# The output norm of a fused decoder layer: three engines or VectorE alone, and one addition moved between two products

## The chip, the cores and the metric

One core of a Trainium2 chip runs the whole layer. The metric is the device time of one execution in microseconds (us); of several runs the median is given. The engines named here: TensorE (PE in the profile; its weight loads are PEld) multiplies, VectorE (DVE), ScalarE (ACT) and POOL (GpSimd) work elementwise, and SP issues the transfers.

## The reference, cut to what matters

The layer projects x (2048 x 2048, float32), runs a convolution branch and an attention branch, concatenates them to y and maps y back. The change touches the last two lines only:

```python
    y = jnp.concatenate([y_conv, y_attn], axis=-1)
    y = jnp.einsum("bse,ed->bsd", y, w_out) + b_out
    return layer_norm(DEEPNORM_ALPHA * x + y, ln_g, ln_b)

def layer_norm(x, g, b):
    mu = jnp.mean(xf, axis=-1, keepdims=True)
    var = jnp.mean(jnp.square(xf - mu), axis=-1, keepdims=True)
    y = (xf - mu) * lax.rsqrt(var + LN_EPS)
    return y * g + b
```

## The kernel before, in words

**Stages.** The sequence is cut into four chunks of 512 rows (`SC`, `NCH`). The list `steps` (L612 to L620) holds 4 x 84 steps of the input projection with its branches, then 112 steps of the output projection. This document is about the latter, called the output stage.

**Products.** The output projection runs by Strassen-like products: two blocks (`blk` 0 and 1) of two chunks each, and for each block seven products in the order 1, 2, 6, 5, 3, 7, 4 (`PRODS`, L33). A product has two halves (`dp` 0 and 1) of four steps (`p` 0 to 3). A step multiplies one 128 x 1024 weight piece with two tiles of y for four row tiles (`tp`): 24 matmuls, since float32 is handled as a high and a low part and each product of parts is its own matmul (`mm3`, L738 to L741). The half `dp` 0 accumulates in the right-hand banks (tiles out_s, out_t, out_v in the profile), `dp` 1 in the left-hand ones (tile out).

**Weights.** SP loads a piece (`wr`) three steps ahead (`load_w(n + 3)`). Two steps ahead `split_w` makes the high part `wh` on ScalarE (L135); the low part `wl` is loaded from DRAM in steps with even p, and in steps with odd p it is computed on POOL by `lo_part` (L138, `wl<-wr,wh`). The pieces of the last three steps are handled by `tail_w` in two halves each.

**Positions and U.** An output tile of 128 x 512 is a position; it starts as `xn`, alpha x + b_out (`scale_xn`, L432), and `evac_out` adds products to it. c11 and c12 belong to the block's first chunk, c21 and c22 to its second. U keeps product 1 (copied on ScalarE) and takes product 6, then product 7 in addition. After product 7 the tile U is added to c21 and c22, and c22 is done; c21 is done after product 4. `z_done` takes a position's statistics (`bn_stats`, L439); c11 is spilled to DRAM there and later loaded again as `zl`. The evacuations of a half are emitted in the first step of the half that follows (`late`, L878 to L883).

**The norm.** `out_norm(c)` (L583) makes 19 background functions for a chunk: one with the small per-row work (`norm_small`, L554) and the first loads, 16 units (one position each, `norm_unit`, L572) and two with the last stores. Function n of a unit also loads the position after next and stores the one before the last. A unit is three operations on three engines: ScalarE scales and shifts the rows (L575), VectorE multiplies by g (L576), POOL adds b (L577). Chunk 0 is started at the first step of product 7 in block 0, chunk 1 at the first step of block 1, chunk 2 at the first step of product 7 in block 1. The fourth chunk has a norm of its own, `tail_norm` (L753 to L783), in the last step.

**What sets the order.** Background functions wait in the queue `bg`; each step of the output stage takes one, or two if its number is a multiple of 4 or more than 18 are queued (L889). All transfers go through SP in the order in which the code emits them (`dma`, L72 to L78), so a store that waits for its data holds back the loads behind it. All 128 x 512 tiles come from one pool of 69 slots (`NSLOT`). The last four steps (from `TAIL`, L621) emit no matmuls until the last one, which runs all four for one row tile after the other, each followed by its evacuation and its norm (L897 to L903).

Of the kernel before, what the change touches and what calls it, by code (L numbers as in the profile page):

```python
# [12 lines left out]
AF = mybir.ActivationFunctionType  # L13
ALU = mybir.AluOpType
# [37 lines left out]
def hybrid_layer_kernel(ctx, tc, x, xT, w_first, w_in, w_out, consts, b_out, ln_g, ln_b, out):  # L52
    nc = tc.nc
    V, A, G, T = nc.vector, nc.scalar, nc.gpsimd, nc.tensor
# [25 lines left out]
    def slot(name, dt=F32):  # L80
        return slots.tile([P, 512], dt, tag="slot", name=name)

    def acc_bank(name):
        return ps_acc.tile([P, 512], F32, tag="acc", name=name)
# [7 lines left out]
    def score_banks(name):  # L92
        sc = ps_sc.tile([P, 2, 512], F32, tag="sc", name=f"{name}_s")
        return [sc[:, 0, :], sc[:, 1, :]]

    def right_banks(name):
        return score_banks(name) + [ps_pt.tile([P, 512], F32, tag="pt", name=f"{name}_t"),
                                    ps_pv.tile([P, 512], F32, tag="pv", name=f"{name}_v")]
# [35 lines left out]
    def copy(dst, src):  # L134
        A.activation(out=dst, in_=src, func=AF.Copy)  # L135
# [37 lines left out]
    bg = deque()  # L173
    later = []
    st = {}

    def run_bg(n):
        for _ in range(min(n, len(bg))):
            bg.popleft()()

    def run_all():
        run_bg(len(bg))
# [251 lines left out]
    def z_done(c, s, d, spill=False):  # L434

        z = st["z", c, s, d] = st.pop(("zx", c, s, d))
        if ("bn", c, s) not in st:
            st["bn", c, s] = small.tile([P, 4, 6], F32, tag="bn", name=f"bn{c}_{s}", bufs=16)
        V.bn_stats(out=st["bn", c, s][:, d, :], in_=z)  # L439
        if spill:  # L440
            t = zd[c, s, d] = dram.tile([P, 512], F32, tag=f"zd{c}_{s}_{d}", name=f"zd{c}_{s}_{d}")
            store_later(t, st.pop(("z", c, s, d)))
# [6 lines left out]
    def add(a, b):  # L449
        V.tensor_tensor(out=a, in0=a, in1=b, op=ALU.add)  # L450

    def evac_out(blk, i, dp, tp):


        ps = st["banks", dp][tp]
        c11, c12, c21, c22 = (2 * blk, tp, dp), (2 * blk, tp, dp + 2), (2 * blk + 1, tp, dp), (2 * blk + 1, tp, dp + 2)
        if i == 1:
            u = st["U", dp, tp] = slot(f"U{blk}_{dp}_{tp}")
            copy(u, ps)
            add(st["zx", *c11], ps)  # L460
        elif i == 2:
            add(st["zx", *c11], ps)
            z_done(*c11, spill=True)
        elif i == 6:
            add(st["U", dp, tp], ps)
            add(st["zx", *c12], st["U", dp, tp])
        elif i == 7:
            u = st.pop(("U", dp, tp))
            add(u, ps)
            add(st["zx", *c21], u)  # L470
            add(st["zx", *c22], u)
            z_done(*c22)
        elif i == 4:
            add(st["zx", *c21], ps)
            z_done(*c21)
        elif i == 5:
            add(st["zx", *c12], ps)
            add(st["zx", *c22], ps)
        else:
            add(st["zx", *c12], ps)  # L480
            z_done(*c12)
# [72 lines left out]
    def norm_small(c, ss):  # L554

        n = len(ss)
        mv = small.tile([P, 4, 2], F32, tag="mv", name=f"mv{c}_{ss[0]}")
        w = small.tile([P, 4, 4], F32, tag="w", name=f"w{c}_{ss[0]}")
        for k, s in enumerate(ss):
            V.bn_aggr(out=mv[:, k, :], in_=st["bn", c, s])  # L560
        V.tensor_scalar(out=w[:, 0, 0:n], in0=mv[:, 0:n, 1], scalar1=EPS, scalar2=None, op0=ALU.add)
        for f in rsqrt_steps(w[:, 0, 0:n], w[:, 1, 0:n], w[:, 2, 0:n]):
            f()
        V.scalar_tensor_tensor(out=w[:, 3, 0:n], in0=mv[:, 0:n, 0], scalar=-1.0, in1=w[:, 1, 0:n],
                               op0=ALU.mult, op1=ALU.mult)
        for k, s in enumerate(ss):
            st["nrm", s] = (w[:, 1, k:k + 1], w[:, 3, k:k + 1])

    def load_gb(c, d):
        st["g", d], st["b", d] = bcast_row(ln_g, d, f"g{c}_{d}"), bcast_row(ln_b, d, f"b{c}_{d}")  # L570

    def norm_unit(c, s, d):  # L572
        z = st["z", c, s, d]
        rstd, nmr = st["nrm", s]
        A.activation(out=z, in_=z, func=AF.Identity, scale=rstd, bias=nmr)  # L575
        V.tensor_tensor(out=z, in0=z, in1=st["g", d], op=ALU.mult)  # L576
        G.tensor_tensor(out=z, in0=z, in1=st["b", d], op=ALU.add)  # L577

    def store(c, s, d):
        r = c * SC + s * P  # L580
# [144 lines left out]
    for j in range(16):  # L725
        job = (j // 8, j // 2 % 4, j % 2)
        n = PER + 10 + 14 * j
# [10 lines left out]
    def mm3(o, lh, ll, mh, ml, start, stop):  # L738
        T.matmul(o, lh, mh, start=start, stop=False)  # L739
        T.matmul(o, lh, ml, start=False, stop=False)  # L740
        T.matmul(o, ll, mh, start=False, stop=stop)  # L741
# [57 lines left out]
    for n, s in enumerate(steps):  # L799
        st["n"] = n  # L800
        c = s[1]
# [4 lines left out]
        if c == 0 and s[0] == "first":  # L806
            i = s[2]
# [20 lines left out]
        if s[0] in ("first", "last"):  # L828
            p = s[2]
            hi, lo = splits[n]  # L830
            if p == 0 and s[0] == "first":
                st["acc"] = [acc_bank(f"in{c}_{i}") for i in range(2)] + score_banks(f"in{c}")
            elif p == 0:
                st["acc"] = right_banks(f"in{c}l")
            for t in range(4):
                for kk in range(2):
                    k = 2 * p + kk
                    xh, xl = xs[c, k]
                    if s[0] == "first":
                        h, l = (w[kk][:, t * P:(t + 1) * P] for w in (hi, lo))  # L840
                    else:
                        h, l = (w[t // 2][:, t % 2 * 256 + kk * P:t % 2 * 256 + kk * P + P] for w in (hi, lo))
                    mm3(st["acc"][t], h, l, xh, xl, k == 0, k == KT - 1)
            if p == 7 and s[0] == "first":
                for t in (2, 3, 1, 0):
                    evac_in(c, t, *ORDER[t], st["acc"][t])
            elif p == 7:
                for t in range(4):
                    evac_in(c, 38 + t, *ORDER[38 + t], st["acc"][t])
                run_all()  # L850
                bg.extend(st["fins"])
            run_bg(2)
        elif s[0] == "in":
            _, c, t, kind, j, hf = s
            hi, lo = splits[n]
            if hf == 0:
                ps = acc_bank(f"in{c}_{t}")
            for k in range(8):
                xh, xl = xs[c, hf * 8 + k]
                cols = slice(k % 4 * P, (k % 4 + 1) * P)  # L860
                mm3(ps, hi[k // 4][:, cols], lo[k // 4][:, cols], xh, xl, hf == 0 and k == 0, hf == 1 and k == 7)
            if hf == 1:
                evac_in(c, t, kind, j, ps)
            run_bg(5)
        else:
            _, blk, i, dp, p = s
            if p == 0:
                st["banks", dp] = (left_banks if dp else right_banks)(f"out{blk}_{i}_{dp}")
            for h, d in NEW.get(i, ()):
                if p == 0:  # L870
                    st["bo", d] = bcast_row(b_out, dp + d, f"bo{blk}_{i}_{dp}_{d}")
                else:
                    scale_xn(2 * blk + h, p - 1, dp + d, st["bo", d])
                load_xn(2 * blk + h, p, dp + d)
            tail = n >= TAIL
            if not tail:
                out_mm(n, range(4))
            for f, *args in late:  # L878
                f(*args)
            late = []  # L880
            if p == 3 and not tail:
                late = [(scale_xn, 2 * blk + h, 3, dp + d, st["bo", d]) for h, d in NEW.get(i, ())]
                late += [(evac_out, blk, i, dp, tp) for tp in range(4)]  # L883
            if dp == 0 and p == 0:
                if i == 7:
                    bg.extend(out_norm(2 * blk))
                elif i == 1 and blk == 1:
                    bg.extend(out_norm(1))
            run_bg(2 if n % 4 == 0 or len(bg) > 18 else 1)  # L889
            if TAIL - 6 <= n < TAIL - 3:  # L890
                tail_w(n + 7)
            if TAIL - 3 <= n < TAIL:
                st["tailw", n + 4]()
                if n == TAIL - 1:
                    for d in range(4):
                        load_gb(3, d)
            if n == len(steps) - 1:  # L897
                run_all()
                for tp in range(4):
                    for m in range(TAIL, TAIL + 4):  # L900
                        out_mm(m, (tp,))
                    evac_out(blk, i, dp, tp)
                    tail_norm(3, tp)  # L903
# [78 lines left out]
```

## Time and profile before

| | |
|---|---|
| median of 3 runs (lowest to highest) | 2689.36 us (2686.81 to 2693.9) |
| the profiled execution | 2691.23 us |
| its span, first to last instruction | 2689.2 us |
| matmuls busy, share of the span | 97% |
| VectorE, ScalarE, POOL busy | 70%, 43%, 32% |
| granted clock of TensorE, mean | 0.991 of full speed |

A duration is that of one instruction; an engine that works without a pause starts the next one somewhat before the end of the one before. "Idle before" is time in which the engine did nothing ahead of the row's instruction, with the instruction that released it. Tile names leave buffer numbers out: out_s, out_t and out_v are accumulation banks of `dp` 0, out those of `dp` 1; wr, wh and wl are a weight piece and its parts; xn and zl are positions that were kept or loaded again; yl is the low part of a tile of y.

### The profile page before, as it was taken

To read this page: it belongs to the slowest core of one execution; us is meant where nothing else is said; L and a number is where in the kernel's file an instruction comes from. 1 tells how busy PE (TensorE), PEld (TensorE's weight loads), DVE (VectorE), ACT (ScalarE), POOL (GpSimd) and SP (SyncE) were. 2 spreads that over 40 slices of the span, in tenths; PEclk is the share of its full clock that TensorE was granted. 3 is DMA by queue.
4 is the path that set the end of the run, shared out by engine and by line. 5 is a ranking of instruction groups with operands and counts; after the bars stand their busy time and mean duration, and the time that the engine had idled before them with its cause. 6 is when DMAs were issued, how large, how long until landed. Compare 5 with 4: busy or idle time off the path is not lost.

```text
span 2689.2 us, 34266 instructions
## 1 busy us (share of the span) xinstructions
PE 2616.0 (97%) x12064; PEld 2175.8 (81%) x12064; DVE 1884.6 (70%) x2992; ACT 1155.9 (43%) x2069; POOL 856.4 (32%) x582
## 2 busy tenths in 40 slices
PE   8999999999999999999999999999999999899985
PEld 7888888788888887888888888888888887678874
DVE  4487788847658757486767747657857768697687
ACT  4344344634444545344454644444444324243241
POOL 2455455312222323122222212312122224352244
PEclk9999999999999999999999999999999999899997
DMA  7655555766755687656766866755568888699894
GB/s 266 190 177 174 174 181 188 249 234 233 234 189 200 211 291 264 212 197 208 242 219 208 298 237 227 239 190 198 192 219 312 315 285 302 201 346 336 275 311 141
DMA packets 238348, 629.51 MB, mean 234 GB/s; under 512 B 26464, under 2 KB 42976, under 8 KB 238176
## 3 DMA queue, kind: packets, MB, share of 16 engines
q1 hardware_dynamic: 238176, 627.32, 68.6%
q8 instruction: 95, 1.56, 0.2%
q14 instruction: 77, 0.63, 0.1%
HBM read 513.97 MB, written 113.25 MB: 233 GB/s over the span
## 4 chain that ended last, share of the span: by engine, by line
PE 54%; DVE 5%; ACT 1%; issue 1%; DMA 1%; POOL 1%; DVEq 0%; SPq 0%; POOLq 0%; ACTq 0%
PE in L741 10%; PE in L740 10%; PE in L739 10%; PE out L740 3%; PE out L741 3%; PE out L739 3%; PE out_s L740 2%; PE out_s L741 2%; PE out_s L739 1%; PE pv L353 1%; DVE xn L450 1%; PE out_t L739 1%; PE out_t L740 1%; PE out_t L741 1%; PE out_v L739 1%
## 5 line engine op out<-in xcount | busy, mean ns | idle before, releaser
L739 PE MATMUL in<-xh,wh 128*128 128x512 f32 x2304 | 903.5, 392 | 9.5 <-ACT xh L135 6.3
L741 PE MATMUL in<-xh,wl 128*128 128x512 f32 x2304 | 898.8, 391 | 3.7 <-DMA wl<-wlo 3.7
L740 PE MATMUL in<-xl,wh 128*128 128x512 f32 x2304 | 899.8, 391 | 0.0
L135 ACT ACTIVATE wh<-wr 128x1024 fp32r<-128x1024 f32 (+1 forms) x452 | 473.0, 1049 | 809.7 <-PE in L740 313.4
L227 DVE SCALAR_TENSOR_TENSOR cv<-h,cst,cv 128x512 f32<-128x512 f32 x896 | 628.6, 747 | 2.4
L739 PEld LDWEIGHTS in<-xh,wh 128*128 128x128 f32 x2304 | 433.5, 188 | 97.5 <-ACT xh L135 7.0
L741 PEld LDWEIGHTS in<-xh,wl 128*128 128x128 f32 x2304 | 433.3, 188 | 95.2 <-DMA wl<-wlo 4.1
L740 PEld LDWEIGHTS in<-xl,wh 128*128 128x128 f32 x2304 | 433.3, 188 | 86.6 <-DVE xl L138 1.1
L138 POOL TENSOR_TENSOR wl<-wr,wh 128x1024 fp32r<-128x1024 f32 (+1 forms) x134 | 329.3, 2461 | 543.3 <-ACT wh L135 419.8
L740 PE MATMUL out<-wl,yh 128*128 128x512 f32 x448 | 175.7, 392 | 11.9 <-POOL wl L138 11.9
L741 PE MATMUL out<-wh,yl 128*128 128x512 f32 x448 | 175.1, 391 | 0.0
L739 PE MATMUL out<-wh,yh 128*128 128x512 f32 x448 | 167.4, 390 | 0.0
L135 ACT ACTIVATE yh<-yr 128x512 fp32r<-128x512 f32 x112 | 69.9, 627 | 218.6 <-DVE yr L514 212.0
L318 ACT ACTIVATE pr<-pr,sm 128x128 f32<-128x128 f32 x256 | 99.6, 390 | 115.3 <-DVE sm L314 115.3
L382 POOL COPY carry<-h 128x30 f32<-128x30 f32 x32 | 6.7, 210 | 444.7 <-DVE h L165 444.7
L138 POOL TENSOR_TENSOR plc<-pmc,phc 128x512 fp32r<-128x512 f32 x64 | 84.8, 1325 | 173.9 <-ACT phc L135 162.0
L400 DVE SCALAR_TENSOR_TENSOR q<-in,cst,q 64x512 fp32r<-64x512 f32 x64 | 48.0, 750 | 128.0 <-ACT q L399 126.8
L138 DVE TENSOR_TENSOR yl<-yr,yh 128x512 fp32r<-128x512 f32 x112 | 104.7, 939 | 40.7 <-ACT yh L135 39.5
L138 POOL TENSOR_TENSOR tl<-tb,th 128x512 fp32r<-128x512 f32 x56 | 79.2, 1428 | 134.7 <-ACT th L135 131.7
L361 DVE TENSOR_TENSOR o<-o,pv 64x256 f32<-64x256 f32 x128 | 53.3, 416 | 82.9 <-ACT o L135 80.8
L740 PEld LDWEIGHTS out<-wl,yh 128*128 128x128 f32 x448 | 84.4, 188 | 32.0 <-POOL wl L138 14.3
L740 PE MATMUL out_s<-wl,yh 128*128 128x512 f32 x224 | 89.3, 399 | 21.2 <-POOL wl L138 21.2
(400 smaller groups left out, 4223.4 us busy)
## 6 DMA issues: line engine op xcount, KB each, us to landing
wr<-in_w_in_dram SPq DMA_DIRECT2D x272, 512.0 KB, 4.7
wl<-wlo SPq DMA_DIRECT2D x252, 512.0 KB, 3.8
yr<-yd SPq DMA_DIRECT2D x192, 256.0 KB, 5.6
wlo<-wl SPq DMA_DIRECT2D x84, 512.0 KB, 5.1
wr<-T SPq DMA_DIRECT2D x61, 512.0 KB, 6.7
wl<-O SPq DMA_DIRECT2D x55, 512.0 KB, 4.9
wr<-in_w_out_dram SPq DMA_DIRECT2D x48, 512.0 KB, 6.3
xr<-in_xT_dram SPq DMA_DIRECT2D x64, 256.0 KB, 5.3
```

What stands on the lines that cost most here:

```text
L135: A.activation(out=dst, in_=src, func=AF.Copy)
L138: eng.tensor_tensor(out=dst, in0=src, in1=hi.bitcast(F32), op=ALU.subtract)
L227: V.scalar_tensor_tensor(out=o, in0=h[:, t:t + SC], scalar=wt(t), in1=a, op0=ALU.mult, op1=ALU.add)
L318: A.activation(out=p3[:, u, :], in_=p3[:, u, :], func=AF.Exp, scale=HD ** -0.5, bias=sm[:, 1, u:u + 1], accum_out=sm[:, 3, u:u + 1])
L353: T.matmul(o, l, m, start=(n == 0), stop=(n == len(mm) - 1))
L361: V.tensor_tensor(out=of[rows], in0=of[rows], in1=pv[rows, kv, :], op=ALU.add)
L382: G.tensor_copy(out=carry[:, j, :], in_=h[:, SC:SC + 30])
L400: V.scalar_tensor_tensor(out=qs[other], in0=ps[rows], scalar=b1[rows], in1=qs[rows].bitcast(F32), op0=ALU.add, op1=ALU.subtract)
L450: V.tensor_tensor(out=a, in0=a, in1=b, op=ALU.add)
L739: T.matmul(o, lh, mh, start=start, stop=False)
L740: T.matmul(o, lh, ml, start=False, stop=False)
L741: T.matmul(o, ll, mh, start=False, stop=stop)
```

## The change

A unit of the norm becomes two operations on VectorE, (z - mean) times g and that times the reciprocal deviation plus b; ScalarE and POOL take no part. The small operation that formed the negated, scaled mean goes. The statistics are kept by chunk and row tile. The addition of U to c21 moves from the evacuation of product 7 to the first four steps of product 4, two positions a step, and U lives until then. A step takes one background function; it takes three if more than 20 are queued, and in all steps of product 4 of block 1.

```diff
--- before.py
+++ after.py
@@ -465,9 +465,8 @@
             add(st["U", dp, tp], ps)
             add(st["zx", *c12], st["U", dp, tp])
         elif i == 7:
-            u = st.pop(("U", dp, tp))
+            u = st["U", dp, tp]
             add(u, ps)
-            add(st["zx", *c21], u)
             add(st["zx", *c22], u)
             z_done(*c22)
         elif i == 4:
@@ -561,20 +560,17 @@
         V.tensor_scalar(out=w[:, 0, 0:n], in0=mv[:, 0:n, 1], scalar1=EPS, scalar2=None, op0=ALU.add)
         for f in rsqrt_steps(w[:, 0, 0:n], w[:, 1, 0:n], w[:, 2, 0:n]):
             f()
-        V.scalar_tensor_tensor(out=w[:, 3, 0:n], in0=mv[:, 0:n, 0], scalar=-1.0, in1=w[:, 1, 0:n],
-                               op0=ALU.mult, op1=ALU.mult)
         for k, s in enumerate(ss):
-            st["nrm", s] = (w[:, 1, k:k + 1], w[:, 3, k:k + 1])
+            st["nrm", c, s] = (mv[:, k, 0:1], w[:, 1, k:k + 1])
 
     def load_gb(c, d):
         st["g", d], st["b", d] = bcast_row(ln_g, d, f"g{c}_{d}"), bcast_row(ln_b, d, f"b{c}_{d}")
 
     def norm_unit(c, s, d):
         z = st["z", c, s, d]
-        rstd, nmr = st["nrm", s]
-        A.activation(out=z, in_=z, func=AF.Identity, scale=rstd, bias=nmr)
-        V.tensor_tensor(out=z, in0=z, in1=st["g", d], op=ALU.mult)
-        G.tensor_tensor(out=z, in0=z, in1=st["b", d], op=ALU.add)
+        mean, rstd = st["nrm", c, s]
+        V.scalar_tensor_tensor(out=z, in0=z, scalar=mean, in1=st["g", d], op0=ALU.subtract, op1=ALU.mult)
+        V.scalar_tensor_tensor(out=z, in0=z, scalar=rstd, in1=st["b", d], op0=ALU.mult, op1=ALU.add)
 
     def store(c, s, d):
         r = c * SC + s * P
@@ -886,7 +882,10 @@
                     bg.extend(out_norm(2 * blk))
                 elif i == 1 and blk == 1:
                     bg.extend(out_norm(1))
-            run_bg(2 if n % 4 == 0 or len(bg) > 18 else 1)
+            if i == 4 and dp == 0:
+                for q in range(2):
+                    add(st["zx", 2 * blk + 1, p, q], st.pop(("U", q, p)))
+            run_bg(3 if blk == 1 and i == 4 or len(bg) > 20 else 1)
             if TAIL - 6 <= n < TAIL - 3:
                 tail_w(n + 7)
             if TAIL - 3 <= n < TAIL:
```

## Rows read from the trace of the kernel before

**Rows 1.** Page, part 1: busy us, share of the span, instructions.

```profile
PE 2616.0 (97%) x12064; PEld 2175.8 (81%) x12064; DVE 1884.6 (70%) x2992; ACT 1155.9 (43%) x2069; POOL 856.4 (32%) x582
```

**Rows 2.** Waits of PE from 2000 us on: total us, times, longest.

```profile
PE out_s L740 <- POOL wl L138: 21.2, 4, 8.3
PE out L740 <- POOL wl L138: 11.9, 6, 2.3
```

**Rows 3.** Matmuls by tile: ns min/median/max, first and last start us.

```profile
L739 PE MATMUL out_s<-wh,yh x224: 388/389/632, 2012.2 to 2641.8; 128*128 128x512 f32 x112
...
L741 PE MATMUL out<-wh,yl x448: 388/389/628, 2034.6 to 2665.4; 128*128 128x512 f32 x150
```

**Rows 4.** Chain that ended last, two marks inside the output stage: start us, us.

```profile
2077.84 0.91 PE out L739 x4
...
2208.40 0.91 PE out L739 x4
```

**Rows 5.** Busy us of each engine in stretches, then clock, DMA share, GB/s.

```profile
2251.90:2303.40 51.50, 41.26 (x170) 32.72 (x168) 51.34 (x61) 16.92 (x22) 28.57 (x15) 0.93 0.81 283
...
2582.40:2631.20 48.80, 41.06 (x171) 32.49 (x169) 48.73 (x56) 17.29 (x23) 25.01 (x15) 0.97 0.96 327
2631.20:2643.90 12.70, 7.99 (x24) 6.36 (x25) 1.27 (x4) 0.00 (x0) 9.58 (x7) 0.73 0.54 165
2643.90:2665.60 21.70, 21.70 (x97) 17.77 (x95) 20.13 (x45) 3.40 (x5) 10.51 (x7) 1.00 0.20 73
```

**Rows 6.** Timeline of PE, one wait: start us, us, idle before.

```profile
2310.37 0.79 PE L740 MATMUL out_s<-wl,yh 128*128 128x512 f32 x1 [8.27 <-POOL wl L138]
```

**Rows 7.** Timeline of POOL, merged: start us, us, idle before.

```profile
2299.71 8.31 POOL L577 TENSOR_TENSOR xn<-xn,b 128x512 f32<-128x512 f32 x4 [10.82 <-DVE xn L576]
2307.99 4.66 POOL L138 TENSOR_TENSOR wl<-wr,wh 128x1024 fp32r<-128x1024 f32 x2
...
2411.54 2.35 POOL L138 TENSOR_TENSOR wl<-wr,wh 128x1024 fp32r<-128x1024 f32 x1 [12.37 <-ACT wh L135]
```

**Rows 8.** Timeline of ACT, the weight copy behind rows 6.

```profile
2296.52 1.06 ACT L135 ACTIVATE wh<-wr 128x1024 fp32r<-128x1024 f32 x1 [8.23 <-PE out_v L741]
```

**Rows 9.** Single lines: duration ns min/median/max, first and last start us.

```profile
L450 DVE TENSOR_TENSOR U<-U,out x16: 673/678/689, 2141.1 to 2624.3; 128x512 f32<-128x512 f32 x16
...
L576 DVE TENSOR_TENSOR xn<-xn,g x32: 672/688/1787, 2273.4 to 2648.0; 128x512 f32<-128x512 f32 x32
...
L577 POOL TENSOR_TENSOR xn<-xn,b x32: 1250/1737/4654, 2275.3 to 2649.8; 128x512 f32<-128x512 f32 x32
...
L777 DVE SCALAR_TENSOR_TENSOR xn<-xn,tmv,g x8: 733/742/1816, 2651.4 to 2675.1; 128x512 f32<-128x512 f32 x8
```

**Rows 10.** Timeline of DVE: one subtraction beside a weight part on POOL.

```profile
2286.61 2.83 DVE L138 TENSOR_TENSOR yl<-yr,yh 128x512 fp32r<-128x512 f32 x1
```

**Rows 11.** The stretches of rows 5, L576 alone (DVE).

```profile
2251.90:2303.40 51.50, 14.48 (x13) 0.93 0.81 283
2582.40:2631.20 48.80, 13.24 (x11) 0.97 0.96 327
```

**Rows 12.** The first of these stretches, L577 alone (POOL).

```profile
2251.90:2303.40 51.50, 20.34 (x12) 0.93 0.81 283
```

**Rows 13.** Timeline of DVE around the last four steps.

```profile
2642.65 1.29 DVE L450 TENSOR_TENSOR xn<-xn,out_s 128x512 f32<-128x512 f32 x2 [11.43 <-PE out_s L741]
2643.85 1.28 DVE L439 BATCH_NORM_STATS2 bn<-xn 128x6 f32<-128x512 f32 x2
...
2649.47 0.69 DVE L450 TENSOR_TENSOR xn<-xn,out 128x512 f32<-128x512 f32 x1 [0.77 <-PE out L741]
...
2682.42 3.08 DVE L779 SCALAR_TENSOR_TENSOR xn<-xn,tw,b 128x512 f32<-128x512 f32 x3
```

**Rows 14.** Waits of the SP queue from 2030 us on: us, times, longest.

```profile
SPq L76 <- POOL zl L577: 27.5, 11, 5.4
...
SPq L76 <- POOL xn L577: 17.1, 4, 15.3
```

## The prediction

> **What bounds the kernel now.** I read the page first: the matmuls are busy for 97% of the span, VectorE for 70%, ScalarE for 43%, POOL for 32% [rows 1]. The reader is to see that only time in which TensorE stands still can be won, and the time after its last matmul.
>
> Next, who TensorE waits for in the output stage: the low parts of weights that POOL computes, ten times, 33.1 us, and nobody else [rows 2]. That is not the whole loss. The stage's first matmul starts at 2012.2 and its last at 2665.4 [rows 3]; two marks of the chain that lie 24 steps apart, in a stretch without waits, give (2208.40 - 2077.84) / 24 = 5.44 us a step [rows 4]. All 112 steps would take 609, and they take 653: **44 us are lost**. The 11 us beyond the waits are restarts and the granted clock, which stands at 0.93, 0.97 and 0.73 in the stretches with waits and at 1.00 in the last one [rows 5].
>
> Then the longest wait, engine by engine. TensorE has gone on at 2310.37 after 8.27 us [rows 6]. ScalarE had the weight's high part at 2296.52 + 1.06 = 2297.6 [rows 8], so POOL could have subtracted before TensorE stopped (2302.1). But POOL's queue holds four additions of L577 ahead of it, which waited for VectorE's products and ran from 2299.71 to 2308.0; only then come the weights [rows 7]. So the norm's third operation stands in front of TensorE's weights.
>
> Last, VectorE in the two stretches of products 7 and 4: busy for 51.3 of 51.5 us and 48.7 of 48.8 [rows 5]. That isn't work alone. Two additions take 1.20 us start to start [rows 13], 0.60 each; 61 and 56 instructions would be 37 and 34 us. The same multiplication takes 0.69 or 1.79 us [rows 9]: beside a 512-column POOL instruction an operation with two SBUF operands is 1.1 us late, and beside a whole weight part (1024 columns) 2.83 - 0.60 = 2.2 us [rows 10]. An addition that reads PSUM never is (0.69 at most) [rows 9].
>
> **The change, part by part.** The sum is made against the profiled execution: 2691.2 us, 2.0 more than its span and 1.9 above the median of the runs shown. 0.3% (8 us) is about what a measurement can tell.
>
> *POOL's 48 additions go.* POOL is left with weight parts, and no wait behind L577 remains. But a weight whose high part itself is late keeps TensorE waiting without L577 too, as at 2411, where POOL had been idle for 12 us and then took 2.35 [rows 7]. That one wait, 2 us, is the lower end of what stays. The upper end is all six waits in the left-hand banks, 12 us [rows 2], which are short like this one. I take 5, nearer to the lower end: the SP queue, which also loads the weights, stood 27.5 and 17.1 us before stores that waited for L577 [rows 14], and as that goes the high parts come earlier. **44 lost, 5 kept: -39 us.**
>
> *ScalarE's 48 activations go*: nothing, it is 57% idle [rows 1]; if it were late, weights would be, and it gets earlier. The small instruction for the negated mean, three times some 0.15 us, goes too: nothing.
>
> *VectorE gets 48 more operations.* A scalar_tensor_tensor with a column operand takes 0.74 [rows 9], 0.66 start to start by the same overlap, so a unit rises from 0.60 to 1.32 us. Against that stands the lateness that L577 causes: in the first stretch 51.3 - 61 x 0.60 = 14.7 us over the work; three weight parts account for 3 x 2.2 = 6.6 of it, the 12 additions [rows 12] for 8.1, or 0.68 each. **Plus 0.72, minus 0.68: a unit costs VectorE about what it costs now.** It stays full in these stretches, but no wait of TensorE is on VectorE [rows 2]: accumulation banks are needed again four steps (21.8 us) after their evacuation starts, and the splits of y lead by at least as much.
>
> The Trainium skill, Perfetto Trace Analysis, section Optimizing Scalar/DVE Operations, says that where VectorE is saturated, offloading to ScalarE or even GPSIMD may make sense, though moving work between GPSIMD and VectorE might not help as they share a port. Its first half speaks against this change; by it the time would be that of rival 3, 2708 us. The rows agree with its second half: 0.69 against 1.79 us.
>
> *The addition per position* moves from product 7's evacuation to product 4's steps: eight instructions of 0.60 for each block, same engine, same count. Evacuations of product 7 shorten by 4 x 0.60 = 2.4 us, off TensorE's path: nothing. Eight U tiles live up to eight steps longer; I count some 63 of 69 slots in use at the fullest step, so nothing, and a few us on SP's loads if that is one batch short.
>
> *The pace.* Units come one a step instead of five in four, and three a step in the last product. Chunk 0's last unit slips into block 1, chunk 1's norm ends five steps later: each under a step of work in stages where VectorE isn't full. Stores, zl loads and g, b loads slip with their units on the SP queue; no transfer is added. SP's stores now wait for VectorE; behind them are weight loads, issued three steps (16.3 us) ahead. That is the second rival. ScalarE's closing of the third chunk at the stage's start slips by one step, needed 56 steps later: nothing.
>
> *The end.* Here the change costs. From product 7's second half to the last four steps VectorE has eight steps, 43.5 us. Its work now: 56 instructions, 11 of them norm [rows 5, 11], leaves 45 x 0.60 = 27.0. After: all of chunk 2's remaining 13 units must come before the last four steps, where two are left over now: 13 x 1.32 = 17.2. Three weight parts and four halves on POOL add between 0 and 3 x 2.2 + 4 x 1.1 = 11.0. Together 44.2 to 55.2, so 0.7 to 11.7 us late. Then come product 4's eight evacuations (4.8 us), and the first tile of the last four steps is there 5.5 us after they start; now VectorE even waits 0.77 for it [rows 13], so nothing can be won there. Late there: 0 to 11 us. From that tile on VectorE is the bound: busy for 20.1 of 21.7 us [rows 5], from 2649.47 to 2685.5 [rows 13] without a wait for TensorE. What it is late there moves the end one to one. I take 8, nearer to the full collision, since now 48.7 - 56 x 0.60 = 15.1 us are lateness. **Plus 8 us.**
>
> Sum: 2691.2 - 44 + 5 + 8 = **2660 us**.
>
> **The rivals.**
> 1. *VectorE keeps up in the end.* For: weight parts often meet evacuations that read PSUM, which they don't delay. Against: the three units a step in product 4. 2691.2 - 44 + 2 + 0 = 2649.
> 2. *The weights stay late.* With the stores now released by VectorE, SP stands before them as long as it stood for POOL. For: VectorE is full where the stores are. Against: units come slower than now, and a store follows its unit by two steps. Half of the 44 us stay: 2691.2 - 22 + 8 = 2677.
> 3. *VectorE becomes the bound: slower.* Both operations of a unit read two SBUF tiles, so POOL's weight parts meet twice as many, come late as now, and the lateness does not fall. Then the 44 us stay, and the 24 units of the two full stretches [rows 11] add 24 x 0.72 = 17 us: 2691.2 + 17 = 2708. It decides once a unit frees less than 0.72 us of lateness and TensorE waits on VectorE. Against: 1.1 us for each collision, and no such wait now. This is where the rule of the Trainium skill, Perfetto Trace Analysis, section Optimizing Scalar/DVE Operations, would lead.
> 4. *It changes nothing that counts*: waits move from L577 to late high parts in full, the end stays, 2691.
>
> **How the numbers follow.** Forecast 0.60, rival 1 0.16, rival 2 0.12, rival 3 0.07, rival 4 0.05. The forecast's own bounds are 2691.2 - 44 + 2 + 0 = 2649 and 2691.2 - 44 + 12 + 11 = 2670. The range runs from 2646 (rival 1 less the 2.5 us by which the fastest run shown lies under the median) to 2680 (rival 2 with as much more); rivals 3 and 4 are outside. Faster by over 0.3% means below 2681: forecast, rival 1 and four fifths of rival 2, 0.85. Within 0.3%: rival 4 and the rest of rival 2, 0.08. Slower: rival 3, 0.07.
>
> **What would show it.** Right: no wait of TensorE on POOL over 3 us; POOL without L577; VectorE's operations in the norm at 0.74, and 2.8 only beside weight parts; the stage's matmuls in under 615 us; the first tile of the last four steps taken some 8 us after it is there. Wrong: TensorE waiting for VectorE or for a weight load behind a store (rivals 3, 2), or no lateness in the end (rival 1). Should the tail be later than 11 us, g and b of the last chunk, whose loads stand behind the last stores on SP, would be the reason to look at.

## The result and the profile after

The changed kernel takes 2660.05 us (median of four runs, 2656.57 to 2660.18), the kernel before, run beside it, 2689.6; the ratio is 0.9886 with a 95% interval of 0.9869 to 0.9903. The forecast was 2660 us. The profiled execution of the changed kernel is the shortest of its four, 2656.57 us with a span of 2654.9; the numbers from the trace below are of that one execution.

The page's first part for the changed kernel answers to [rows 1]:

```profile
PE 2608.2 (98%) x12064; PEld 2171.8 (82%) x12064; DVE 1881.6 (71%) x3037; ACT 1122.9 (42%) x2021; POOL 780.8 (29%) x534
```

VectorE is as busy as before in total (1881.6 against 1884.6 us) though it now runs all of the norm's operations on the rows (45 instructions more); POOL has 76 us less, ScalarE 33.

The waits of TensorE from 2000 us on, which answer to [rows 2] (total us, times, longest):

```profile
PE out L735 <- ACT wh L135: 3.0, 1, 3.0
PE out L736 <- DMA wl<-O: 1.8, 1, 1.8
PE out_s L736 <- POOL wl L138: 1.0, 1, 1.0
PE out L736 <- POOL wl L138: 0.9, 1, 0.9
```

Ten waits of 33.1 us on POOL have become two of 1.9. Two waits of 4.8 us are new; both lie at the start of the last four steps, on the weight's high part and on a low part that is loaded.

The first and last matmuls of the output stage, as in [rows 3]:

```profile
L735 PE MATMUL out_s<-wh,yh x224: 388/389/462, 2010.5 to 2598.7; 128*128 128x512 f32 x112
...
L737 PE MATMUL out<-wh,yl x448: 387/389/628, 2034.2 to 2630.3; 128*128 128x512 f32 x150
```

From 2010.5 to 2630.3 are 619.8 us, where 112 steps of 5.44 need 609: 11 us are lost instead of 44. Most of that lies at the last four steps: the last matmul ahead of them starts at 2600.53 (timeline of TensorE), and 2600.7 - 2010.5 - 108 x 5.44 leaves 2.7 for everything before.

Busy time in the stretches of products 7 and 4, in the order of [rows 5] (PE, PEld, DVE, ACT, POOL, then clock, DMA share, GB/s): the eight steps of product 7's second half and product 4's first half in block 0, the same eight in block 1 (they end where the last four steps begin), the wait, the last four:

```profile
2249.70:2293.20 43.50, 43.50 (x194) 36.03 (x193) 42.92 (x58) 14.14 (x18) 13.60 (x5) 1.00 0.97 355
2557.00:2600.50 43.50, 43.50 (x193) 36.01 (x192) 43.46 (x57) 10.76 (x14) 12.00 (x6) 1.00 0.84 303
2600.50:2603.90 3.40, 0.41 (x2) 0.00 (x0) 3.40 (x5) 2.32 (x3) 2.37 (x2) 1.00 0.98 355
2603.90:2630.60 26.70, 24.87 (x96) 19.77 (x96) 25.17 (x50) 3.40 (x5) 8.68 (x6) 0.87 0.54 191
```

TensorE is busy all through both stretches at full clock, and VectorE still has no pause in them: 42.9 and 43.5 of 43.5 us. Of these rows only the last has a lowered clock, 0.87, and TensorE had just stood still for 3 us ahead of it.

The timeline of VectorE around the last four steps answers to [rows 13]; the first row shows two operations of the norm beside POOL's weight parts:

```profile
2602.55 3.45 DVE L572 SCALAR_TENSOR_TENSOR xn<-xn,mv,g 128x512 f32<-128x512 f32 x2
...
2609.90 1.27 DVE L450 TENSOR_TENSOR xn<-xn,out_s 128x512 f32<-128x512 f32 x2
...
2615.13 0.69 DVE L450 TENSOR_TENSOR xn<-xn,out 128x512 f32<-128x512 f32 x1 [0.39 <-PE out L737]
...
2648.09 3.08 DVE L775 SCALAR_TENSOR_TENSOR xn<-xn,tw,b 128x512 f32<-128x512 f32 x3
```

The last four steps could have begun at 2010.5 + 108 x 5.44 + 2.7 = 2600.7 and their first tile been added 5.5 us later. It is added at 2615.13, **8.9 us late**, after VectorE had waited 0.39 us for its last matmul, and from there to the end of VectorE's work it takes 36.0 us, as long as before.

The timeline of the SP queue shows why the weights were late there too (start us, us; a merged row holds the wait between its transfers):

```profile
2585.37 10.58 SPq L76 DMA_DIRECT2D out_dram<-zl  x2
2596.01 1.41 SPq L76 DMA_DIRECT2D wr<-T  x3
2597.51 3.61 SPq L76 DMA_DIRECT2D out_dram<-xn  x3
2601.21 0.38 SPq L76 DMA_DIRECT2D wl<-O  x1
```

Two stores of zl hold the queue for 10.6 us, until VectorE has finished the second of them (2593.81 + 1.78 = 2595.59, from its timeline); only then are the last weights loaded.

### The profile page after: what moved, and what is told of

The parts are those of the page before. It is cut to its first block, busy times and chain, and to the rows that moved or that the text cites. A ratio compares the mean times of both kernels' runs of the same rounds, so it can differ in the third digit from the quotient of the medians.

```text
span 2654.9 us, 34199 instructions
## 1 busy us (share of the span) xinstructions
PE 2608.2 (98%) x12064; PEld 2171.8 (82%) x12064; DVE 1881.6 (71%) x3037; ACT 1122.9 (42%) x2021; POOL 780.8 (29%) x534
## 4 chain that ended last, share of the span: by engine, by line
PE 56%; DVE 4%; DMA 1%; ACT 1%; issue 0%; POOL 0%; SPq 0%; DVEq 0%; ACTq 0%; POOLq 0%
PE in L737 10%; PE in L736 10%; PE in L735 10%; PE out L736 3%; PE out L737 3%; PE out L735 3%; PE out_s L736 2%; PE out_s L737 2%; PE out_s L735 2%; PE pv L353 1%; PE out_v L735 1%; PE out_v L737 1%; PE out_t L737 1%; PE out_t L735 1%; PE out_t L736 1%; PE out_v L736 1%
## 5 line engine op out<-in xcount | busy, mean ns | idle before, releaser
L138 POOL TENSOR_TENSOR wl<-wr,wh 128x1024 fp32r<-128x1024 f32 (+1 forms) x134 | 334.1, 2495 | 659.4 <-ACT wh L135 513.0
L138 POOL TENSOR_TENSOR plc<-pmc,phc 128x512 fp32r<-128x512 f32 x64 | 84.8, 1325 | 173.9 <-ACT phc L135 146.9
L138 POOL TENSOR_TENSOR tl<-tb,th 128x512 fp32r<-128x512 f32 x56 | 78.9, 1422 | 135.5 <-ACT th L135 132.6
L138 DVE TENSOR_TENSOR yl<-yr,yh 128x512 fp32r<-128x512 f32 x112 | 93.3, 836 | 32.3 <-ACT yh L135 31.1
L735 PEld LDWEIGHTS out<-wh,yh 128*128 128x128 f32 x448 | 84.6, 189 | 21.1 <-ACT wh L135 3.4
```

Source lines behind the costliest of these rows:

```text
L138: eng.tensor_tensor(out=dst, in0=src, in1=hi.bitcast(F32), op=ALU.subtract)
```

## The experiments

Twelve kernels ran, each beside the kernel before, whose median was 2689.6 to 2692.4 us in the four groups of runs; so medians of different groups compare only to within some 3 us, and the ratios are the safer column. e2 and e8 leave a part of the norm out; they price that part, and what they compute is not the layer. The last column is a measure that does not depend on the stages ahead, whose end lies between 2010.5 and 2016.7 us in these profiles: from the start of the output stage's first matmul to the addition of the first tile of the last four steps (L450, `xn<-xn,out`), both read from the profiles. From that addition to the end of the span it is 39.7 us before and 39.8 after.

| run | median us | ratio to before, 95% | first matmul to first tile, us |
|---|---|---|---|
| before | 2689.6 | | 637.2 |
| the change | 2660.05 | 0.9869 to 0.9903 | 604.6 |
| e1 b on VectorE | 2669.48 | 0.9906 to 0.9939 | 617.1 |
| e2 without b | 2656.22 | 0.9856 to 0.9885 | 601.2 |
| e3 only the addition moved | 2688.8 | 0.9985 to 1.0003 | 635.2 |
| e4 only the pace | 2682.1 | 0.9951 to 0.9979 | 626.9 |
| e5 change, old pace | 2664.91 | 0.9885 to 0.9918 | 611.3 |
| e6 change, weights first | 2661.73 | 0.9875 to 0.9905 | 604.1 |
| e7 change, two a step in product 7 | 2657.51 | 0.9859 to 0.9888 | 603.1 |
| e8 change, one operation in chunk 2 | 2653.46 | 0.9845 to 0.9874 | 597.3 |
| e9 change, product 4's low parts loaded | 2659.97 | 0.9870 to 0.9899 | 606.0 |
| e10 e9 with e6 and e7 | 2663.41 | 0.9879 to 0.9913 | 609.9 |
| e11 change, addition moved back | 2662.24 | 0.9876 to 0.9906 | 604.7 |
| e12 before, product 4's low parts loaded | 2676.06 | 0.9930 to 0.9959 | 623.0 |

### Whose waits they were: e1, e2, e12

**e1**, on the kernel before:

```diff
-        G.tensor_tensor(out=z, in0=z, in1=st["b", d], op=ALU.add)
+        V.tensor_tensor(out=z, in0=z, in1=st["b", d], op=ALU.add)
```

> The kernel before with one edit: the norm's third operation, the addition of b, runs on VectorE instead of POOL (ScalarE keeps the first, the pace and the addition per position stay). Theory (TensorE's waits were POOL's queue, in which L577 stood in front of the weights): the ten waits of 33 us shrink to under 8 us, 2655 to 2668 us. Rival (the new pace or the later addition per position made the difference): 2680 us or more. Rival (VectorE bound): slower than before, 2700.

2669.48 us, 1.5 above the range. The waits of TensorE in its output stage (total us, times, longest):

```profile
PE out_s L740 <- DMA wl<-O: 5.3, 3, 2.6
PE out L740 <- DMA wl<-O: 3.4, 1, 3.4
PE out L740 <- POOL wl L138: 2.0, 1, 2.0
```

With L577 off POOL, POOL's part of the waits falls from 33.1 to 2.0 us. But 8.7 us of waits for loaded low parts take their place. The stores on SP, ahead of loads, now wait for VectorE's additions (29.0 and 13.8 us on `xn` and `zl` of L577 by the waits of SP); that is no more than the 44.6 us that SP stood for POOL's [rows 14], and why it reaches TensorE only here is not shown. And the first tile of the last four steps comes 14.2 us after they start instead of 5.6, since two units of the norm stand ahead of it on VectorE and wait for g:

```profile
2625.54 1.29 DVE L576 TENSOR_TENSOR xn<-xn,g 128x512 f32<-128x512 f32 x2 [5.85 <-DMA g<-in_ln_g_dram]
```

The last loads of g and b were issued from 2613.41 on, right behind two stores that had held SP's queue for 5.42 us. So the queue on POOL was the cause of the waits, and two smaller costs that were behind it come out.

**e2** takes that line out and puts nothing in its place.

> The kernel before without the addition of b for the first three chunks: b is left out there, nothing replaces it. Theory: TensorE's waits go as in the run with b on VectorE, and VectorE has 48 operations of 0.6 us less than there, which shows only at the end, where VectorE is late: 2646 to 2658 us, 0 to 10 less than with b on VectorE. Rival (VectorE's load sets the time of the full stretches): 25 us or more less than with b on VectorE.

2656.22 us, 13.3 less than e1: more than the theory's 0 to 10, about half of the rival's 25. Here the last four steps' first tile comes 5.6 us after they start, as before, so 8.6 us of the 13.3 are the end, and 5.9 of these were e1's wait for g; most of the rest is the waits for loaded low parts, 3.0 us here against 8.7. VectorE's work is not what sets the time of the full stretches; what it has too much is paid in the end and, as far as the rows go, through the stores that it releases late.

**e12** leaves the norm on three engines and takes POOL's weight parts away instead: the low parts of product 4 are made during the input projection and loaded, for odd p too (e9 has the same edit on the changed kernel).

```diff
-           for i in range(1, 8) for q in pieces if q[1] % 2 == 0}
+           for i in range(1, 8) for q in pieces if q[1] % 2 == 0 or i == 4}
...
-        return n >= PER and (steps[n][0] != "out" or steps[n][4] % 2 == 0)
+        return n >= PER and (steps[n][0] != "out" or steps[n][4] % 2 == 0 or steps[n][2] == 4)
...
-        if p % 2 == 0:
+        if p % 2 == 0 or i == 4:
```

> The kernel before with all low weight parts of product 4 loaded from DRAM; the norm stays on three engines. Theory (TensorE's long waits were the weights' place in POOL's queue behind L577): the four long waits in the right-hand banks, 21 us, vanish although L577 still collides with VectorE; 2664 to 2678 us. Rival (VectorE's lateness by collisions is what holds TensorE): other waits take their place, 2684 us or more.

2676.06 us, in the theory's range. The waits of TensorE in its output stage:

```profile
PE out L740 <- POOL wl L138: 14.2, 6, 3.6
PE out_s L740 <- DMA wl<-O: 5.0, 2, 4.6
PE out L739 <- ACT wh L135: 1.6, 1, 1.6
```

The 21.2 us of waits on POOL in the right-hand banks [rows 2] are gone, with L577 still on POOL and still colliding with VectorE (L576 on `xn` takes 1772 ns in the median there, 688 in [rows 9]); 6.6 us of waits for loaded low parts and for a high part came in. The waits in the left-hand banks, which belong mostly to other products, stay (14.2 us). That separates the queue from the collisions for the four long waits: it was the place in POOL's queue.

### The other two parts of the change: e3, e4, e5, e11

**e3** has only the moved addition on the kernel before; **e11** takes only that back from the changed kernel.

```diff
-            u = st.pop(("U", dp, tp))
+            u = st["U", dp, tp]
             add(u, ps)
-            add(st["zx", *c21], u)
...
+            if i == 4 and dp == 0:
+                for q in range(2):
+                    add(st["zx", 2 * blk + 1, p, q], st.pop(("U", q, p)))
```

> The kernel before with the addition per position moved from product 7 to product 4 and nothing else. Theory: same engine, same count, off TensorE's path: 2685 to 2694 us, the ten waits behind L577 stay at 25 to 40 us. Rival (the shorter evacuation of product 7 relieves VectorE where it is full, so L577 gets its data earlier): 2680 or less.

> The changed kernel with the addition per position back in product 7's evacuation. Theory: the same sum of VectorE work in the same eight steps: 2657 to 2663 us. Rival (the move is what lets VectorE keep up): 2665 us or more.

2688.8 us, its interval holding 1, and 2662.24 against 2660.05, with ranges of single runs that overlap (2658.47 to 2663.31 and 2656.57 to 2660.18); the first tile comes at 604.7 instead of 604.6 us, and e11's stage starts 5.9 us later in its profile. The move does nothing that these runs can tell.

**e4** has only the pace on the kernel before; **e5** is the changed kernel with the old pace.

```diff
-            run_bg(2 if n % 4 == 0 or len(bg) > 18 else 1)
+            run_bg(3 if blk == 1 and i == 4 or len(bg) > 20 else 1)
```

> The kernel before with the new pace of background functions and nothing else. Theory: L577 still stands in front of POOL's weights, 2680 to 2700 us, waits of TensorE on POOL between 20 and 45 us. Rival (the pace spreads the norm and so frees the weights): 2670 or less.

> The changed kernel with the pace of before (one function a step, two in every fourth step or above 18 queued). The pace alone gave some 8 us on the kernel before. Theory (the pace spaces stores, so that weight loads don't stand behind stores that wait for VectorE, and ends the norm before the last four steps): 2663 to 2671 us, with one to three waits of TensorE of 1 to 4 us for weight loads, and two units of the norm left over in the last steps. Rival (the pace matters only where L577 fills POOL's queue): 2657 to 2662.

The pace alone gives 0.35%, with TensorE's waits on POOL at 23.1 us instead of 33.1 (in its longest run of five, 2676.82 to 2685.15), inside the theory's ranges for both: L577 still stands in front. On the changed kernel the old pace costs 4.9 us by the medians; the intervals of the two ratios overlap, the single runs do not, and the first tile comes 6.7 us later. Its waits are small (5.9 us in four, none over 2.3); what is late is the first tile, 16.5 us after the last four steps begin, since two units are left over. They stand ahead of the first tile on VectorE and wait for a transfer there:

```profile
2623.07 1.41 DVE L572 SCALAR_TENSOR_TENSOR xn<-xn,mv,g 128x512 f32<-128x512 f32 x2 [4.36 <-DMA g<-in_ln_g_dram]
2624.40 1.41 DVE L573 SCALAR_TENSOR_TENSOR xn<-xn,w,b 128x512 f32<-128x512 f32 x2
2625.72 0.68 DVE L450 TENSOR_TENSOR xn<-xn,out 128x512 f32<-128x512 f32 x1
```

The first row begins after 4.36 us of waiting for g, whose load stands behind the last stores on SP: the place that the prediction named should the tail be later than 11 us. So the pace is worth 5 to 8 us, more than I had given it. e1 and e5, both with the old pace, differ by ScalarE's operation and the moved addition, 2669.48 against 2664.91; no run takes ScalarE's operation off alone, and their intervals overlap.

### What makes the end late: e6, e7, e8, e9, e10

**e6** moves the last weight loads ahead of the stores on SP:

```diff
+            if TAIL - 6 <= n < TAIL - 3:
+                tail_w(n + 7)
+            if n == TAIL - 4:
+                list(load_w(TAIL))
+            if n == TAIL - 3:
+                load_lo(TAIL)
...
             run_bg(3 if blk == 1 and i == 4 or len(bg) > 20 else 1)
-            if TAIL - 6 <= n < TAIL - 3:
-                tail_w(n + 7)
```

> The changed kernel with the weight loads of the last four steps issued ahead of the stores of the norm on the SP queue. Theory (VectorE, over its budget in product 4, sets the end): TensorE no longer waits at the start of the last four steps, the first tile's addition still starts at nearly the same time, total 2656 to 2661 us. Rival (the end is late because those weights stand behind stores): the first tile is taken 7 to 9 us earlier, 2653 us or less.

2661.73 us. Its waits of TensorE in the output stage, and the addition of the first tile on VectorE:

```profile
PE out_s L736 <- POOL wl L138: 1.1, 1, 1.1
PE out L736 <- POOL wl L138: 0.9, 1, 0.9
```

```profile
2617.89 0.67 DVE L450 TENSOR_TENSOR xn<-xn,out 128x512 f32<-128x512 f32 x1
```

The total is 0.7 above the theory's range; the stage starts 3.3 us later in this profile, and VectorE waits 1.4 us for g after the first tile (0.4 in the changed kernel). The place of the first tile is what tells. TensorE no longer waits at the start of the last four steps, 2604.4 there; yet the first tile is added 13.5 us later, and VectorE waits for no matmul there. From the stage's start that is 604.1 us against 604.6. So the two new waits of the changed kernel cost the 0.4 us that VectorE waits there and no more: VectorE's lateness sets the end, and the weights' lateness is nearly as large beside it.

**e8** leaves out the second operation of a unit in chunk 2:

```diff
+        if c != 2:
             V.scalar_tensor_tensor(out=z, in0=z, scalar=rstd, in1=st["b", d], op0=ALU.mult, op1=ALU.add)
```

> The changed kernel without the second operation of a unit in chunk 2: the product with the reciprocal deviation and the addition of b are left out there. Theory (VectorE is over budget by some 8 us in product 4): 13 operations of 0.66 us less put it back in time; the first tile of the last four steps is taken when TensorE has it, 2650 to 2654 us. Rival (VectorE's load is not what makes the end late): 2658 to 2661.

2653.46 us, as expected: the first tile comes 7.0 us after the last four steps begin (5.6 in the kernel before), and those begin without a wait. From there to the end it takes 2.5 us longer than in the changed kernel, in part since g of the last chunk arrives late (VectorE waits 1.8 us for it, 0.4 there).

**e7** takes two functions a step in product 7 of block 1:

```diff
-            run_bg(3 if blk == 1 and i == 4 or len(bg) > 20 else 1)
+            run_bg(3 if blk == 1 and i == 4 or len(bg) > 20 else 2 if blk == 1 and i == 7 else 1)
```

> The changed kernel with two functions a step instead of one in product 7 of block 1, so that chunk 2's units and loads come earlier. Theory (VectorE's sum of work sets the end): only its idle time before that can be won, some 3 us: 2655 to 2660 us. Rival (stores come earlier and hold back weight loads while VectorE is full): waits of TensorE for weights of 3 us or more, 2662 to 2668.

2657.51 us: both were right in part. VectorE is earlier, but four waits of TensorE for weights in products 7 and 4, 1.0 to 1.8 us each, make the last four steps begin 7 us later than they might, so VectorE waits for the first tile again, 0.9 us. The gain of 2.5 us on the change is within the runs' ranges, 2654.70 to 2659.43; no run here that computes the whole norm beats the change clearly.

**e9** puts e12's edit on the changed kernel; **e10** adds e6 and e7 to it.

> The changed kernel with all low weight parts of product 4 loaded from DRAM (those of odd p too, made during the input projection), so that POOL computes nothing in product 4. Theory (VectorE is late in the end, in part by its collisions with POOL's weight parts there): without the collisions of two weight parts and four halves, up to 8.8 us, the first tile is taken 3 to 9 us earlier: 2651 to 2657 us. Rival (the collisions don't count, or the added loads hold TensorE up): 2659 us or more.

> As the run with product 4's low parts from DRAM, and the weight loads of the last four steps ahead of the stores, and two functions a step in product 7 of block 1. Theory: VectorE uses 2 to 3 us of idle time more and TensorE's weights are not behind stores: 2648 to 2655 us. Rival (the transfers become the bound in product 7): 2657 us or more, with waits of TensorE for weights.

2659.97 and 2663.41 us: the rivals were right about the time. VectorE did come earlier, as its waits around the last four steps show for e9:

```profile
DVE xn L450 <- PE out_s L737: 4.5, 1, 4.5
DVE xn L450 <- PE out L737: 1.7, 1, 1.7
```

It waits 6.2 us for matmuls; in the changed kernel 0.4 of the same kind. But now TensorE is late, by waits of 1.8 and 0.8 us for loaded low parts and 2.6 for a high part from 2580 us on. The transfers in the stretch of product 7 and 4 (2555 to 2610 us) of e9, then those of the changed kernel (2557 to 2605):

```profile
DMA packets 9165, 20.66 MB, mean 376 GB/s; under 512 B 1020, under 2 KB 1020, under 8 KB 9161
...
q1 hardware_dynamic: 9161, 20.61, 102.3%
```

```profile
DMA packets 6691, 14.83 MB, mean 309 GB/s; under 512 B 741, under 2 KB 741, under 8 KB 6687
...
q1 hardware_dynamic: 6687, 14.78, 84.6%
```

The mean rate rises from 309 to 376 GB/s with the DMA engines busy all the time, and SP no longer stands before a store of zl for VectorE (0.3 us from 2540 us on, where the changed kernel has one of 9.6). So the rows fit a bound that has moved to the transfers; no run shows that apart. What VectorE would gain without those loads stays open; it wasn't tried.

## Why the prediction was right

**What bounds it.** The 44 us that TensorE lost were the place to look, and the queue on POOL was the cause of its waits: e1 and e12 take L577 or the weights out of that queue, by different edits, and the waits go in the places where the theory has them.

**The term for POOL** (44 lost, 5 kept) measured 2.7 kept up to the last four steps. The lower end, 2, was nearer: with L577 gone, SP stands 23.8 us before stores that wait for the norm (L573, by its waits from 2030 us on) instead of 44.6 [rows 14], and nearly all high parts come in time.

**VectorE's units.** An operation of the norm takes 0.74 us (median of L572 and L573, as of L777 in [rows 9]), the longest 2.89, beside a weight part. The stretches stayed full, 42.9 and 43.5 of 43.5 us, and TensorE waited for nothing in them. The balance of plus 0.72 and minus 0.68 a unit comes out of the two traces, by sums over the output stage: the norm's operations took 54.3 us before (48) and 89.9 after (96), 0.74 a unit more; the other operations with two SBUF operands, the subtractions of L138 on VectorE, the sums of y (L514, now L513), L432 and the additions of U, 283.2 us before and 253.4 after in equal numbers, 0.62 a unit less.

**The end** (plus 8, between 0 and 11) measured 8.9, and e6 and e8 show the reason that was given: VectorE over its budget. TensorE's weights were late there by nearly as much, which the forecast's term did not have.

**The sum** by these measured terms is 2691.2 - 44 + 2.7 + 8.9 = 2658.8. The profiled execution took 2656.6; 1.7 of the difference lie ahead of the stage, whose first matmul starts at 2010.5 instead of 2012.2. Set like against like, one profiled execution against the other, the forecast was 3.4 us too long. The median is 3.5 above that execution, so that the forecast meets the median is luck; that it lies within a few us is not.

**The signs.** No wait of TensorE on POOL is over 1.0 us, L577 is off POOL, and the first tile comes 8.9 us late, as said. Of the signs of being wrong one came too: 4.8 us of waits for weights whose loads stood behind stores. The sign that failed is "the stage's matmuls in under 615 us": they took 619.8, since the last four steps began 3.4 us late for a weight and then took 26.7 us instead of 21.7 [rows 5], with another wait of 1.8 and the clock at 0.87. I had looked for lateness there on VectorE alone.

**What was wrong in it.** "The pace" was costed at nothing but slips of a step, and it is worth 5 to 8 us: e4 shows 10 us of TensorE's waits on POOL less, e5 two units left over that wait for g, where the new pace ends the norm in time. Both lie inside the terms that were summed, the waits and the end, so the sum did not show it. And rival 2 was not wrong everywhere: weights do come late behind stores that wait for VectorE, by 8.7 us in e1 and 4.8 in the changed kernel, where VectorE is full anyway.

**The rule.** The Trainium skill, Perfetto Trace Analysis, section Optimizing Scalar/DVE Operations, says that where VectorE is saturated, offloading some work from it may make sense, and cautions that GPSIMD and VectorE share a port. The trace does not bear out the first for this kernel: ScalarE's and POOL's parts of the norm went onto a full VectorE, and the kernel got faster by 1.1%. It agrees with the caution: VectorE's busy time in total did not rise with 45 instructions more (1884.6 and 1881.6 us). What decided the time was neither, but which instruction stood ahead of TensorE's weights in POOL's queue, as e1 and e12 show.

## What to carry to other kernels

A wait that the profile puts down to an engine may be a place in that engine's queue: look at what ran just ahead, and at when the input was there. Before moving the work, price the engine that takes it where it is full, at its own distances and with its collisions, and look for the point at which its lateness is paid, which here was the last four steps. Once one bound goes, the next is close: the runs that ease VectorE, the stores in front of weight loads, or both (e6 to e10) all lie between 597.3 and 609.9 us in the table, around the 604.6 of the change.

## What the runs showed of the hardware

The collision between VectorE and POOL reaches tiny operations as well. Three operations of 128 x 4 elements out of one chain, the first and the last the same line (timeline of VectorE in the changed kernel), and POOL's weight part there:

```profile
2541.75 0.16 DVE L150 TENSOR_TENSOR w<-w 128x4 f32<-128x4 f32 x1
...
2542.35 0.16 DVE L153 TENSOR_TENSOR w<-w 128x4 f32<-128x4 f32 x1
2542.54 2.25 DVE L150 TENSOR_TENSOR w<-w 128x4 f32<-128x4 f32 x1
```

```profile
2542.35 2.42 POOL L138 TENSOR_TENSOR wl<-wr,wh 128x1024 fp32r<-128x1024 f32 x1 [8.49 <-ACT wh L135]
```

It takes 0.16 us alone and 2.25 beside a weight part. That is no single case: of this line's nine operations in the output stage six took 0.15 to 0.17 us, and the three that took 2.25 to 2.34 each began within 0.2 us after a weight part on POOL. It is the POOL instruction that sets the price, 2.25 - 0.16 = 2.1 us, about the 2.2 that a subtraction of 512 columns lost in [rows 10], not the size of the operation. So in small chains on VectorE one collision can cost as much as the whole chain.

Operations with one operand in an accumulation bank did not meet it, as the prediction took from 16 additions: in the kernel before, none of the 128 additions of L450 that read a bank took over 0.69 us, while those of U, with both operands in SBUF, took up to 2.82. Two of these groups (ns min/median/max, first and last start us):

```profile
L450 DVE TENSOR_TENSOR xn<-xn,out x48: 664/681/689, 2067.5 to 2672.3; 128x512 f32<-128x512 f32 x48
L450 DVE TENSOR_TENSOR xn<-xn,U x48: 666/682/2823, 2121.2 to 2629.3; 128x512 f32<-128x512 f32 x48
```
